# One decoder layer on one core: weight differences skipped at three token groups, a score bank for one group of transposes, output weight casts moved behind mixer parts

## The chip, the cores and the metric

The kernel runs on one core of a Trainium2 chip (trn2). The metric is the device time of one execution in microseconds (us). Five engines work side by side, each through its own instructions in a fixed order: PE (TensorE, matrix products), DVE (VectorE), ACT (ScalarE), POOL (GpSimd) and SP (SyncE, which here issues all the DMA transfers). An engine that must wait for another stands still, with everything that is queued behind the waiting instruction.

## The reference

The layer takes 1024 tokens of width 1024, puts 16 meta tokens ahead of them and computes, in fp32:

```python
h = concatenate([meta, x])                       # 1040 x 1024
a = rmsnorm(h, ln_mix_pre)
dq, dk, dv, hq, hf, hi, hg = split(a @ w_in)     # 28 column tiles of 128
y_diff = diff_attention(dq, dk, dv, ...)         # 4 heads, two softmaxes each: p0 - lam * p1, times v
y_hgrn = hgrn2(hq, hf, hi, hg, ...)              # 4 heads, gated linear recurrence with decay f
h = h + rmsnorm(concatenate([y_diff, y_hgrn]) @ w_out, ln_mix_post)
u = conv3(rmsnorm(h, ln_ffn_pre) @ w_up) + b     # causal convolution over 3 tokens, 2 x 2816 channels
h = h + rmsnorm((gelu(u[gate]) * u[up]) @ w_down, ln_ffn_post)
return h[16:]
```

## The kernel before

Each fp32 operand of a product is split into a rounded high part (a cast on ACT) and the low remainder (a subtraction on DVE or POOL), and three products stand for one: high x high, high x low, low x high. The tokens lie in 9 blocks (block 0 has 16 tokens, the others 128), in three groups of three blocks.

The mixer part runs head by head. PE's instructions keep the order in which the program writes them; the other engines' instructions are ordered by the scheduler. For head h, `interleave` (L57) mixes two streams. The dense stream (`dense`, L755) computes projections: for each column tile and each token group 24 products (8 slices of 128 rows, three products each). The side stream is either attention of head h (`attn`) or the recurrence of head h (`hgrn_head`). So there are two kinds of phase: in the first, four tiles of the recurrence's projections (hf, hq, hi, hg) run beside attention; in the second, with `wide` set, three tiles of the next head's attention projections (dq, dk, dv) run beside the recurrence.

Before each token group, `dense` also takes one step of a second side stream, `down_sums` (L194). It prepares differences of blocks of w_down for a Strassen-like product much later: for each of 11 slices it loads four 256 KB tiles (tag "wd", five buffers), and makes four subtractions on DVE (tiles named wd3, wd12, wd22, wd21), each followed by a store to a DRAM scratch tensor, tsc. A slice takes six steps: two that only pass time and four with a subtraction. All 11 slices take 66 steps; the loops offer 4 x 12 steps in the first kind of phase and 3 x 9 in the second, 75.

In attention, `scores(i)` makes the products S (two PSUM banks, tag "S", two such pairs) and for the last block also E (tag "m", two single banks). ACT exponentiates them into pb. `values(i)` turns the difference of the two softmaxes, pb, by PE transposes: four 128 x 128 blocks go to one PSUM tile, pt, in bank tag "m" (L695), and are copied to SBUF as at (by DVE for even pieces, by ACT for odd ones); the first key block goes to az. `apply(i)` multiplies them with v into pa (tag "m"). Blocks 4 to 7 have two such pieces, block 8 has three.

In the recurrence, DVE multiplies decay factors into q (kept in the mix tiles) and k (tile kr) level by level, PE makes the products of each level (pl), and after level 7 PE transposes kr (pk, L518) for the state update.

After the last head, `out_first` (L1036) computes the first half of the output projection while the recurrence of head 3 runs beside it: for token block i, the mixer parts mm (k slices 0 to 3 and 4 to 6) are split and multiplied with the weights wo0 into py, copied to y0. Beside that, the raw weights of the second half (wor1_k) are loaded and split (`load_wo`) into high (wh1 or woh1, ACT) and low (wl1 or wol1, DVE). The raw weights of the first half, wor0_3 to wor0_7, and those of the second half use the five "wd" buffers that the weight differences had.

Its order around the change, before:

```python
for n, i in enumerate(FIRST[2:]):
    for w in [nxt.pop(0) for _ in range((2, 2, 1, 1, 1, 1)[n])]:
        with tc.issue_after(V.last.ins):
            wo.append(load_wo(*w))
```

Here `issue_after` keeps an instruction behind a named one in the scheduler's order; `V.last` and `A.last` are the last DVE and ACT instructions written so far. SP issues its DMAs strictly in its own order, so a store that waits for DVE holds back every load behind it.

Of the kernel before, what the change touches and what calls it, by code (L numbers as in the profile page):

```python
# [26 lines left out]
NBLK = 9  # L27
# [10 lines left out]
def start(i):  # L38
    return 0 if i == 0 else META + P * (i - 1)


def rows(i):
    return META if i == 0 else P
# [44 lines left out]
def layer_kernel(ctx: ExitStack, tc: tile.TileContext, x, meta, table, lbl, gpre, gpost, win,  # L88
# [3 lines left out]
    V, A = Ordered(tc, nc.vector, state), Ordered(tc, nc.scalar, state)  # L92
# [56 lines left out]
    def ps_m(name):  # L149
        return pp.tile([P, 512], F32, tag="m", name=name)  # L150

    def ps_s(name):
        return pp.tile([P, 2, 512], F32, tag="S", name=name)

    def split(hi, lo, raw, eng=None):
        A.copy(hi, raw)
        (eng or G).tensor_tensor(lo, raw, hi.bitcast(F32), op=ALU.subtract)
# [18 lines left out]
    def mix(ks, t0, t1):  # L176
        g = 0 if t1 <= start(3) else 1 if t1 <= start(6) else 2
        base = start(GROUPS[g][0])
        return mixes[g][:, ks, t0 - base:t1 - base]
# [48 lines left out]
    def load_m(m, name, where=None, bufs=4):  # L228
        return [load_split(win[m][:, 512 * c: 512 * (c + 1)], f"{name}_{c}", where, bufs) for c in range(2)]

    def proj_group(g, parts, name, evac, wide=False):
        b0, b1 = GROUPS[g]
        t0, t1 = start(b0), start(b1 - 1) + P
        n = t1 - t0
        pt = ps_s(f"pi_{name}_{g}")[:, 0] if wide and g == 2 else ps_in(f"pi_{name}_{g}")
        for k in range(KD):
            yield from proj_step(pt[:, :n], parts, k, t0, t1, lambda: evac(g, b0, b1, t0, t1, pt[:, :n]))
# [171 lines left out]
    def flush():  # L409
        while late:  # L410
            to_nat(*late.pop(0))
# [212 lines left out]
    def attn(h, tens):  # L624
# [61 lines left out]
        def values(i):  # L686
            r = rows(i)
            q0 = start(i)
            W = q0 + r
            nm = f"{h}_{i}"  # L690
            pb = pend.pop(i)
            pieces = [list(range(j, min(j + 4, i + 1))) for j in range(0, i + 1, 4)]
            ats = []
            for pi, blks in enumerate(pieces):
                pt = ps_m(f"pt{nm}_{pi}")  # L695
                at = ap_.tile([P, len(blks) if pi == 2 else 4, P], F32, tag=f"at{pi // 2}", name=f"at{nm}_{pi}", bufs=2 - pi // 2)
                for jj, j in enumerate(blks):
                    b = rows(j) if i == 0 else P
                    T.transpose(pt[:b, jj * r:(jj + 1) * r], pb[:r, 0, start(j):start(j) + b], ident[:r, :r])
                pv = pt.rearrange("p (j q) -> p j q", j=4)[:, :, :r] if r == P else None  # L700
                n0 = len(blks)
                if pi == 0:
                    A.copy(az[i % 2][:META, :r], pt[:META, :r])
                lo = 1 if pi == 0 else 0
                if n0 > lo:
                    with tc.issue_after(pend["low"].ins) if i == NBLK - 2 else nullcontext():
                        (A.copy if pi % 2 else V.tensor_copy)(at[:, lo:n0], pv[:, lo:n0])
                ats.append(at)
                yield 0.8 if i < 4 else 0.6
            pend["ats"] = ats, pieces  # L710
# [47 lines left out]
    def dense(tiles, preload=None, side=iter(()), wide=False):  # L758
        parts = preload
        for idx, (m, name, evac) in enumerate(tiles):  # L760
            if parts is None:
                parts = load_m(m, name)
            nxt = load_m(tiles[idx + 1][0], tiles[idx + 1][1]) if idx + 1 < len(tiles) else None
            for g in range(3):
                next(side, None)
                for step, c in enumerate(proj_group(g, parts, name, evac, wide)):
                    if step == 8:
                        flush()
                    yield c
            parts = nxt  # L770
# [28 lines left out]
    pt = ps_m("pg")  # L799
# [146 lines left out]
    def load_wr(n, k):  # L946
        raw = (wp.tile([P, 512], F32, tag="wr", name=f"wor{n}_{k}", bufs=3) if n == 0 and k < 3
               else wsp.tile([P, 512], F32, tag="wd", name=f"wor{n}_{k}"))
        last_load.append(SY.dma_start(raw, wout[P * k: P * (k + 1), 512 * n: 512 * (n + 1)]))
        return n, k, raw  # L950

    def load_wo(n, k, raw):
        if k < 2:
            where, tag, bufs = wp, ("wh", "wl"), 4
        elif n == 0 and k < KD - 1:
            where, tag, bufs = w0p, ("woh", "wol"), KD - 3
        else:
            where, tag, bufs = w1p, ("woh", "wol"), KD - 1
        hi, lo = (where.tile([P, 512], F32R, tag=t, name=f"{t}{n}_{k}", bufs=bufs) for t in tag)
        split(hi, lo, raw, V if n or k else G)  # L960
        return hi, lo

    def tok(i):
        return (2, 14) if i == 0 else (P, start(i))

    def mix_split(i, k0, k1):
        r, t0 = tok(i)
        src = mix(slice(k0, k1), t0, t0 + r)
        if i < 2:
            hi, lo = (kept[:, 0, k0:k1], kept[:, 1, k0:k1]) if i else (m0[:, k0:k1, 0:2], m0[:, k0:k1, 32:34])  # L970
        elif k1 - k0 == 1:
            m = mlp.tile([P, 2, 1, P], F32R, tag="m1", name=f"mm{i}_{k0}", bufs=7)
            hi, lo = m[:, 0], m[:, 1]
        else:
            m = map_.tile([P, 2, k1 - k0, P], F32R, tag="mm", name=f"mm{i}_{k0}")
            hi, lo = m[:, 0], m[:, 1]
        A.copy(hi, src)
        V.tensor_tensor(lo, src, hi.bitcast(F32), op=ALU.subtract)
        if i > 1 and k1 < KD:
            for c in range(k0 // 2, (k1 + 1) // 2):  # L980
                ka, kb = max(k0, 2 * c), min(k1, 2 * c + 2)
                SY.dma_start(msc[i, c][:, :, P * (ka - 2 * c):P * (kb - 2 * c)],
                             m[:, :, ka - k0:kb - k0].bitcast(F32).rearrange("p l k t -> p l (k t)"))
        return hi, lo, k0, k1, r

    def out_part(sp_, py, wo, first, last, ks=None):
        mh, ml, k0, k1, r = sp_
        for k in ks or range(k0, k1):
            hi, lo = wo[k]
            j = k - k0  # L990
            T.matmul(py[:r], mh[:, j, :r], hi, start=(first and j == 0), stop=False)  # L991
            yield 216
            T.matmul(py[:r], mh[:, j, :r], lo, start=False, stop=False)
            yield 216
            T.matmul(py[:r], ml[:, j, :r], hi, start=False, stop=(last and k == k1 - 1))
            yield 216
# [12 lines left out]
    wo = []  # L1009
# [29 lines left out]
    def out_first():  # L1039
        pys = [ps_s(f"py0_{i}")[:, 0] for i in FIRST[:2]]  # L1040
        for ks in ((0, 1), (2, 3)):
            for j in range(2):
                yield from out_part(sps[j], pys[j], wo0, ks[0] == 0, False, ks)
        sqs = [mix_split(i, 4, 7) for i in FIRST[:2]]
        for j in range(2):
            yield from out_part(sqs[j], pys[j], wo0, False, True)
            if j == 0:
                sp_ = mix_split(FIRST[2], 0, 4)
            A.copy(y0[:, FIRST[j]], pys[j])
        nxt = [load_wr(1, k) for k in range(4)]  # L1050
        for n, i in enumerate(FIRST[2:]):
            for w in [nxt.pop(0) for _ in range((2, 2, 1, 1, 1, 1)[n])]:
                with tc.issue_after(V.last.ins):
                    wo.append(load_wo(*w))
            nxt += [load_wr(1, k) for k in ((4,), (5,), (6,), (7,), (), ())[n]]
            if n == 3:
                ahead.extend(mix_load(2, c) for c in range(4))
            py = ps_in(f"py0_{i}")
            sq_ = mix_split(i, 4, 7)
            yield from out_part(sp_, py, wo0, True, False)  # L1060
            if i != FIRST[-1]:
                sp_ = mix_split(FIRST[n + 3], 0, 4)
            yield from out_part(sq_, py, wo0, False, True)
            A.copy(y0[:, i], py)
        py = ps_in("py0_0")
        yield from out_meta(py, wo0, 0, 7, 6)
        A.copy(y0[:2, 0], py[32:34])
        V.tensor_tensor(y0[:2, 0], y0[:2, 0], py[:2], op=ALU.add)
        while 0 not in finished:
            yield None  # L1070
        for p in range(3):
            pre_last[p] = mix_split(p, 7, 8)
        for p in range(3):
            yield from out_last(p)
# [172 lines left out]
    for n, i in enumerate(order):  # L1247
# [9 lines left out]
        nxt = []  # L1257
# [507 lines left out]
```

## Time and profile before

| what | value |
|---|---|
| median of 3 runs | 1296.62 us (1295.83 to 1296.99) |
| the profiled execution | 1296.41 us, of which 1294.6 us from the first instruction to the last |
| PE busy | 1269.1 us (98%), so 25.5 us of idle |
| DVE, ACT, POOL busy | 916.8 us (71%), 689.2 us (53%), 408.7 us (32%) |
| granted TensorE clock | 0.999 |
| mixer with projections | up to about 514 us |
| output projection, first half beside recurrence 3 | about 514 to 576 us |

The page gives, for each group of instructions, its busy time, the mean duration and the idle time of its engine just before, with what ended it. In the timeline a row is: start, length, engine, line, operation, output<-inputs, shape, count, and in brackets the idle time of the engine before it and the instruction whose end released it. Helper functions carry most DVE and ACT instructions, so these rows have L54, and one reads them by their tile names.

### The profile page before, as it was taken

How to read it: one execution, taken by the hardware profiler on the slowest of the kernel's cores; microseconds unless marked ns; L12 is line 12 of the kernel's file. 1: busy time of each engine (PE TensorE's matmuls, PEld its weight loads, DVE VectorE, ACT ScalarE, POOL GpSimd, SP SyncE). 2: the span in 40 equal slices, each digit the busy share in tenths (PEclk: the TensorE clock that was granted, in tenths of full speed). 3: DMA queues.
4: the chain of work that ended last, by engine and by line, in shares of the span. 5: the costliest groups of instructions: out<-in, count | busy, mean ns of one | idle time of the engine just before them, and what ended most of it. 6: DMA issues, size and time to landing. Idle time of an engine off the chain costs nothing.

```text
span 1294.6 us, 26319 instructions
## 1 busy us (share of the span) xinstructions
PE 1269.1 (98%) x10236; PEld 1181.0 (91%) x10236; DVE 916.8 (71%) x1581; ACT 689.2 (53%) x1672; POOL 408.7 (32%) x322
## 2 busy tenths in 40 slices
PE   7999999999999999999999999999999999999997
PEld 6899999999999999777899999999999998888886
DVE  7566657575757565737887787787787786697587
ACT  7465347544654566446666455455445454454454
POOL 3211212021212020022154766766766730010020
PEclk9999999999999999999999999999999999999999
DMA  6222323122323311727612322222222236955363
GB/s 222 92 89 66 105 76 115 54 99 98 99 86 100 98 42 32 259 102 233 223 58 83 106 83 81 83 83 76 85 86 75 84 103 216 343 197 171 90 211 122
DMA packets 84371, 153.07 MB, mean 118 GB/s; under 512 B 9571, under 2 KB 19843, under 8 KB 84246
## 3 DMA queue, kind: packets, MB, share of 16 engines
q1 hardware_dynamic: 84246, 151.39, 35.1%
q8 instruction: 80, 1.31, 0.4%
q14 instruction: 45, 0.37, 0.1%
HBM read 112.69 MB, written 38.67 MB: 117 GB/s over the span
## 4 chain that ended last, share of the span: by engine, by line
PE 53%; DVE 2%; ACT 1%; DMA 0%; issue 0%; DVEq 0%; SPq 0%
PE pd L1576 5%; PE pd L1577 5%; PE pd L1575 5%; PE pb L1376 4%; PE pb L1377 4%; PE pb L1378 4%; PE pa L1377 3%; PE pa L1376 3%; PE pa L1378 3%; PE pc L1376 3%; PE pc L1378 3%; PE pc L1377 3%; PE pq L1353 2%; PE pq L1354 2%; PE pq L1355 2%; PE py L991 1%
## 5 line engine op out<-in xcount | busy, mean ns | idle before, releaser
L1376 PE MATMUL pb<-t,uh 128*128 128x258 f32 (+1 forms) x456 | 127.4, 279 | 0.7 <-DVE u L54 0.7
L1377 PE MATMUL pb<-t,uh 128*128 128x258 f32 (+1 forms) x456 | 127.3, 279 | 0.0
L1378 PE MATMUL pb<-t,ul 128*128 128x258 f32 (+1 forms) x456 | 127.2, 279 | 0.0
L1576 PE MATMUL pd<-wl,gh 128*128 128x512 f32 (+1 forms) x314 | 120.7, 384 | 0.4 <-DVE wl L54 0.3
L1577 PE MATMUL pd<-wh,gl 128*128 128x512 f32 (+1 forms) x314 | 120.9, 385 | 0.0
L1575 PE MATMUL pd<-wh,gh 128*128 128x512 f32 (+1 forms) x314 | 120.6, 384 | 0.0
L54 DVE SCALAR_TENSOR_TENSOR c<-uu,cwt,c 128x512 f32<-128x512 f32 x88 | 95.0, 1079 | 22.3 <-ACT c L54 21.4
L1325 POOL TENSOR_TENSOR c<-c,c 128x512 f32<-128x512 f32 x44 | 64.5, 1465 | 127.4 <-ACT c L54 108.6
L54 DVE SCALAR_TENSOR_TENSOR c<-ug,cwt,c 128x512 f32<-128x512 f32 x88 | 84.0, 955 | 6.6 <-ACT c L54 5.9
L1376 PEld LDWEIGHTS pb<-t,uh 128*128 128x128 f32 x456 | 85.8, 188 | 1.1 <-DVE u L54 1.1
L1377 PEld LDWEIGHTS pb<-t,uh 128*128 128x128 f32 x456 | 85.9, 188 | 0.0
L1378 PEld LDWEIGHTS pb<-t,ul 128*128 128x128 f32 x456 | 85.8, 188 | 0.0
L1377 PE MATMUL pa<-t,uh 128*128 128x256 f32 (+1 forms) x304 | 85.3, 281 | 0.0
L1378 PE MATMUL pa<-t,ul 128*128 128x256 f32 (+1 forms) x304 | 85.2, 280 | 0.0
L1376 PE MATMUL pa<-t,uh 128*128 128x256 f32 (+1 forms) x304 | 85.2, 280 | 0.0
L1378 PE MATMUL pc<-t,ul 128*128 128x256 f32 x304 | 83.9, 276 | 0.0
L1376 PE MATMUL pc<-t,uh 128*128 128x256 f32 x304 | 83.9, 276 | 0.0
L1377 PE MATMUL pc<-t,uh 128*128 128x256 f32 x304 | 83.9, 276 | 0.0
L1576 PEld LDWEIGHTS pd<-wl,gh 128*128 128x128 f32 x314 | 58.9, 188 | 13.8 <-DVE wl L54 1.5
L1577 PEld LDWEIGHTS pd<-wh,gl 128*128 128x128 f32 x314 | 59.0, 188 | 11.9
L1575 PEld LDWEIGHTS pd<-wh,gh 128*128 128x128 f32 x314 | 59.0, 188 | 11.8
L54 ACT ACTIVATE c<-ug,cbt,cwt 128x512 f32<-128x512 f32 x44 | 35.9, 816 | 44.0 <-issue 26.2
(411 smaller groups left out, 4289.3 us busy)
## 6 DMA issues: line engine op xcount, KB each, us to landing
ra<-in_wup_dram SPq DMA_DIRECT2D x76, 256.0 KB, 2.6
wd<-in_wdown_dram SPq DMA_DIRECT2D x44, 256.0 KB, 3.2
tsc<-wd SPq DMA_DIRECT2D x44, 256.0 KB, 2.2
gsc<-c SPq DMA_DIRECT2D x44, 256.0 KB, 2.0
wi<-tsc SPq DMA_DIRECT2D x44, 256.0 KB, 2.9
gi<-gsc SPq DMA_DIRECT2D x33, 256.0 KB, 3.7
wi<-in_wdown_dram SPq DMA_DIRECT2D x33, 256.0 KB, 3.3
msc<-mm SPq DMA_DIRECT2D x21, 256.0 KB, 3.3
```

Source lines behind the costliest of these rows:

```text
L54: ins = call(*args, **kw)
L991: T.matmul(py[:r], mh[:, j, :r], hi, start=(first and j == 0), stop=False)
L1325: G.tensor_tensor(cg, cg, cu, op=ALU.mult)
L1353: T.matmul(pt, hi[:, s], th[:, k], start=(kh + k == 0), stop=False)
L1354: T.matmul(pt, hi[:, s], tl[:, k], start=False, stop=False)
L1355: T.matmul(pt, lo[:, s], th[:, k], start=False, stop=(kh == 1 and k == 3))
L1376: T.matmul(pt, hi[:, s], th[:, k], start=(first and k == 0), stop=False, skip_group_check=True)
L1377: T.matmul(pt, hi[:, s], tl[:, k], start=False, stop=False, skip_group_check=True)
L1378: T.matmul(pt, lo[:, s], th[:, k], start=False, stop=(k == 3), skip_group_check=True)
L1575: T.matmul(py, gh[:, s], wh, start=(k == 0 and pr not in (3, 7)), stop=False, skip_group_check=True)
L1576: T.matmul(py, gh[:, s], wl, start=False, stop=False, skip_group_check=True)
L1577: T.matmul(py, gl[:, s], wh, start=False, stop=(k == NH - 1), skip_group_check=True)
```

## The change

There are three edits. First, in the second kind of phase (`wide`), `dense` takes no step of the weight differences before the token groups numbered 4, 5 and 6 of 9. This takes nine steps out of 75 and leaves the 66 that are needed, so the differences end with the last token group of head 3's first kind of phase. Second, the transposes of piece 1 of block 7 (NBLK - 2) go into the first half of a score pair (tag "S") and no longer into an "m" bank. Third, in `out_first` the splits of the second half's weights are written behind the next block's mixer part and behind the first products of the present block, and are kept behind the last DVE and the last ACT instruction; the loads of wor1_4 to wor1_7 are written earlier by one or more blocks in the table of loads.

```diff
-                pt = ps_m(f"pt{nm}_{pi}")
+                pt = ps_s(f"pt{nm}_{pi}")[:, 0] if (i, pi) == (NBLK - 2, 1) else ps_m(f"pt{nm}_{pi}")
...
             for g in range(3):
-                next(side, None)
+                if not (wide and 4 <= 3 * idx + g <= 6):
+                    next(side, None)
                 for step, c in enumerate(proj_group(g, parts, name, evac, wide)):
...
         for n, i in enumerate(FIRST[2:]):
-            for w in [nxt.pop(0) for _ in range((2, 2, 1, 1, 1, 1)[n])]:
-                with tc.issue_after(V.last.ins):
-                    wo.append(load_wo(*w))
-            nxt += [load_wr(1, k) for k in ((4,), (5,), (6,), (7,), (), ())[n]]
+            nxt += [load_wr(1, k) for k in ((), (4, 5), (6, 7), (), (), ())[n]]
...
             yield from out_part(sp_, py, wo0, True, False)
             if i != FIRST[-1]:
                 sp_ = mix_split(FIRST[n + 3], 0, 4)
+            for w in [nxt.pop(0) for _ in range((2, 2, 1, 1, 1, 1)[n])]:
+                with tc.issue_after(V.last.ins), tc.issue_after(A.last.ins):
+                    wo.append(load_wo(*w))
             yield from out_part(sq_, py, wo0, False, True)
```

Three places show how the instructions move. The last number in each name is a running buffer number. The first place is PE's order in attention of head 1, around piece 1 of block 7 (pt1_7_1) and the products that use it (pa1_7). Before, with the waits of each instruction:

```order
L247 MATMUL pi_hg1_0_3011<-ahi0_106,wl_hg1_0_2740 128x272 [waits Pool_49]
L699 MATMUL pt1_7_1_3015<-ident_73,pb1_7_2830 128x128 [waits DVE_49]
L699 MATMUL pt1_7_1_3015<-ident_73,pb1_7_2830 128x128 x3
...
L724 MATMUL pa1_7_3027<-avn1_1587,az1_130 128x128 [waits Activation_49]
L724 MATMUL pa1_7_3027<-avn1_1587,at1_7_0_2992 128x128 x3
L724 MATMUL pa1_7_3027<-avn1_1587,at1_7_1_3016 128x128 [waits Activation_49]
```

Now:

```order
L247 MATMUL pi_hg1_0_2998<-ahi0_106,wl_hg1_0_2729 128x272 [waits Pool_49]
L699 MATMUL pt1_7_1_3002<-ident_73,pb1_7_2824 128x128 x4
...
L724 MATMUL pa1_7_3014<-avn1_1587,az1_130 128x128 [waits DVE_49]
L724 MATMUL pa1_7_3014<-avn1_1587,at1_7_0_2986 128x128 x3
L724 MATMUL pa1_7_3014<-avn1_1587,at1_7_1_3003 128x128 [waits Activation_49]
```

The order of the products is the same; the transposes pt1_7_1 no longer wait for DVE, and pa1_7 waits for DVE where it waited for ACT.

The second place is DVE's order in the recurrence of head 0, levels 6 and 7, ahead of PE's transposes of kr. Before:

```order
L54 TENSOR_TENSOR kl1_126<-pi_dk1_1_1973,k1_1_1586 64x384
L54 TENSOR_TENSOR wd21_2_1620<-wd21_2_1620,wd22_2_1618 128x512
L54 COPY am_736<-pl0_6_2053 32x8x32 x2
L54 TENSOR_TENSOR mix0_99<-mix0_99,tt0_1638 128x2x64
L54 TENSOR_TENSOR mix1_100<-mix1_100,tt0_1638 128x3x64
L54 TENSOR_TENSOR kr0_739<-kr0_739,tt0_1638 128x8x64
L54 TENSOR_TENSOR mix2_101<-mix2_101,tt0_1638 128x3x64
```

Now:

```order
L54 TENSOR_TENSOR kl1_126<-pi_dk1_1_1971,k1_1_1586 64x384
L54 COPY am_736<-pl0_6_2049 32x8x32 x2
L54 TENSOR_TENSOR mix0_99<-mix0_99,tt0_1638 128x2x64
L54 TENSOR_TENSOR mix1_100<-mix1_100,tt0_1638 128x3x64
L54 TENSOR_TENSOR kr0_739<-kr0_739,tt0_1638 128x8x64
L54 TENSOR_TENSOR mix2_101<-mix2_101,tt0_1638 128x3x64
L54 COPY am_736<-pl0_7_2087 64x8x64
L54 TENSOR_TENSOR kl0_125<-pi_dk1_2_2044,k0_1_1585 64x384
L54 TENSOR_TENSOR kl1_126<-pi_dk1_2_2044,k1_1_1586 64x384
L54 TENSOR_TENSOR wd22_2_1618<-wd22_2_1618,wd12_2_1616 128x512
```

The difference wd21_2 is gone from ahead of the copies am and the products with mix and kr; another one, wd22_2, comes behind kl, and wd21_2 itself later still.

The third place is the output projection. ACT's order there, before:

```order
L54 CAST woh1_6_6934<-wor1_6_6767 128x512
L54 COPY y0_6308<-py0_4_6562 128x512
L54 CAST mm6_4_6770<-mix2_101 128x384
L54 CAST mm7_0_6829<-mix2_101 128x512
L54 CAST woh1_7_7013<-wor1_7_6871 128x512
L54 COPY y0_6308<-py0_5_6690 128x512
L54 CAST mm7_4_6882<-mix2_101 128x384
```

Now:

```order
L54 CAST woh1_3_6749<-wor1_3_6550 128x512
L54 COPY y0_6308<-py0_4_6552 128x512
L54 CAST mm6_4_6768<-mix2_101 128x384
L54 CAST mm7_0_6827<-mix2_101 128x512
L54 CAST woh1_4_6832<-wor1_4_6678 128x512
L54 COPY y0_6308<-py0_5_6682 128x512
L54 CAST mm7_4_6878<-mix2_101 128x384
```

At the same point among the mixer parts ACT now casts weight 4 where it cast weight 7. And SP's order at the end of head 3's attention, before:

```order
L212 DMA tsc_93<-wd21_10_5285 128x512
L949 DMA wor0_6_6346<-in_wout_dram 128x512
L949 DMA wor0_7_6348<-in_wout_dram 128x512
L163 DMA wr_hg3_1_5896<-in_win_dram 128x512
L949 DMA wor0_0_6334<-in_wout_dram 128x512
```

Now:

```order
L212 DMA tsc_93<-wd22_10_5889 128x512
L950 DMA wor0_5_6344<-in_wout_dram 128x512
L212 DMA tsc_93<-wd21_10_5891 128x512
L950 DMA wor0_6_6346<-in_wout_dram 128x512
L950 DMA wor0_7_6348<-in_wout_dram 128x512
L934 DMA gpo0_6312<-in_gpost_dram 128x512
L983 DMA msc_94<-mm2_0_6350 256x1x256 x2
```

The last weight differences and the loads of wor0_6 and wor0_7 now stand behind all loads of head 3's projection weights, directly ahead of the output projection's own transfers; on DVE the subtraction of wd21_10 now stands behind the gate of the last projection tile's second token group.

## The prediction

> **What bounds the kernel now.** I read the page's busy times first, then PE's waits, then the timelines around the three edits.
>
> ```profile
> span 1294.6 us, 26319 instructions
> PE 1269.1 (98%) x10236; PEld 1181.0 (91%) x10236; DVE 916.8 (71%) x1581; ACT 689.2 (53%) x1672; POOL 408.7 (32%) x322
> ```
>
> PE is idle for 1294.6 - 1269.1 = 25.5 us in all, and it keeps its order and its products. So the change can only move idle time of PE: it gains where a wait goes, and loses where a new one comes. The waits of PE by line (total us, times, longest) that stand at the three edits:
>
> ```profile
> PE pk L518 <- DVE kr L54: 2.4, 2, 1.2
> PE pt L699 <- DVE at L54: 2.3, 4, 1.0
> PE pl L456 <- DVE kr L54: 0.6, 1, 0.6
> PE pl L462 <- DVE mix L54: 0.2, 1, 0.2
> ```
>
> Together that is 5.5 us, the most that the change can give.
>
> **The score bank.** The transposes of piece 1 of block 7 wait once in each head, until DVE has copied piece 0 (at) out of the bank that they reuse. PE's rows of heads 0 and 1 (head 2 has the rest of the 2.3 beside head 3's row further down, 0.52):
>
> ```profile
> 119.68 0.66 PE L699 MATMUL pt<-ident,pb 128*128 128x128 f32 x4 [0.24 <-DVE at L54]
> ...
> 246.49 0.66 PE L699 MATMUL pt<-ident,pb 128*128 128x128 f32 x4 [0.52 <-DVE at L54]
> ...
> 247.94 1.73 PE L724 MATMUL pa<-avn,at 128*128 128x128 f32 x14
> ```
>
> In a bank of its own this wait is gone, but the products pa behind still need the copy of piece 1, which ACT makes, and ACT doesn't get to it earlier: it is busy with an exponential until then.
>
> ```profile
> 246.81 0.66 ACT L54 ACTIVATE pb<-E,ast 128x512 f32<-128x512 f32 x1
> 247.47 0.56 ACT L54 COPY at<-pt 128x512 f32<-128x512 f32 x1
> ```
>
> The copy ends at 247.47 + 0.56 = 248.03. Of the 14 products pa, six use piece 0; the seventh stands at 247.94 + 6 x 1.73/14 = 248.68. Moved 0.52 earlier it would start at 248.16, so 0.13 us of room is left and head 1 keeps all of its 0.52. I take the same for head 2, and all of the 0.24 in head 0, where less is moved. In head 3 more is moved:
>
> ```profile
> 497.24 0.66 PE L699 MATMUL pt<-ident,pb 128*128 128x128 f32 x4 [1.03 <-DVE at L54]
> 498.10 0.58 ACT L54 COPY at<-pt 128x512 f32<-128x512 f32 x1
> 498.59 0.61 PE L724 MATMUL pa<-avn,at 128*128 128x128 f32 x4
> ```
>
> The seventh product stands at about 498.59 + 6 x 0.12 = 499.31, the copy ends at 498.68 plus a hand-over that I put at 0.1; so 0.53 of the 1.03 is gained and a wait of 0.5 on ACT is left. **Term 1: 0.24 + 0.52 + 0.52 + 0.53 = 1.81 us**, with bounds of 0 (the copies decide everywhere) and 2.31.
>
> **The differences left out.** A subtraction of the weight differences (wd) stands in DVE's queue just ahead of the work that PE's transposes pk wait for. Head 0, DVE and then PE:
>
> ```profile
> 166.96 1.35 DVE L54 TENSOR_TENSOR wd<-wd,wd 128x512 f32<-128x512 f32 x1
> 168.34 0.85 DVE L54 COPY am<-pl 32x256 f32<-32x256 f32 x2
> 169.22 1.63 DVE L54 TENSOR_TENSOR mix<-mix,tt 128x128 f32<-128x128 f32 x2
> 170.77 0.68 DVE L54 TENSOR_TENSOR kr<-kr,tt 128x512 f32<-128x512 f32 x1
> ...
> 171.50 0.55 PE L518 MATMUL pk<-ident,kr 128*128 128x128 f32 x3 [1.20 <-DVE kr L54]
> ```
>
> Two of these rows are stretched, and POOL's rows say why: its weight splits run at the same time.
>
> ```profile
> 166.49 1.27 POOL L157 TENSOR_TENSOR wl_hf<-wr_hf,wh_hf 128x512 fp32r<-128x512 f32 x1 [11.03 <-ACT wh_hf L54]
> 169.15 1.28 POOL L157 TENSOR_TENSOR wl_hf<-wr_hf,wh_hf 128x512 fp32r<-128x512 f32 x1 [1.39 <-ACT wh_hf L54]
> ```
>
> Without wd the copies am start at 166.96 and end at 167.81. The mix pair follows, for which I take 0.56 us from head 1 (next fence), to 168.37, and kr with 0.68 ends at 169.05. Without its wait pk would have come at 171.50 - 1.20 = 170.30, so 1.25 us of room is left, and kr would be through before POOL's second split at 169.15, with 0.78 between the two starts. Head 1 shows the chain where POOL doesn't meet it:
>
> ```profile
> 294.55 0.56 DVE L54 TENSOR_TENSOR mix<-mix,tt 128x128 f32<-128x128 f32 x2
> 295.02 0.69 DVE L54 TENSOR_TENSOR kr<-kr,tt 128x512 f32<-128x512 f32 x1
> 296.00 0.49 PE L518 MATMUL pk<-ident,kr 128*128 128x128 f32 x3
> ```
>
> Here pk has no wait. Heads 0 and 2 have the two waits of the list above; **term 2: 2 x 1.20 = 2.40 us**, with bounds of 0 (kr meets POOL and another operation) and 2.40. The number of subtractions is unchanged; nine of the steps fall elsewhere, most into attention. There DVE has pauses, as just behind the copy of at in head 1:
>
> ```profile
> 247.60 0.16 DVE L54 TENSOR_TENSOR ast<-ast 128x1 f32<-128x1 f32 x1 [1.16 <-ACT pb L54]
> ```
>
> A subtraction stands there now; 0.68 fits into 1.16, and I cost it at nothing. With POOL beside it, it would take 1.35, 0.19 more than the pause: over three heads, at most 0.6 us.
>
> The Trainium skill (SBUF — State Buffer, section "SBUF: two separate sides") says that DVE and POOL share a pair of ports as an exclusive lock: an operation of DVE with two SBUF inputs and one of POOL don't share it, and whichever starts first keeps it to its end. The 1.35 for wd against 0.68 for kr agrees. By this rule alone the order of starts decides, and the 0.78 between kr and POOL's split would be all that protects term 2.
>
> **The casts in the output projection.** ACT stands behind the load of wor1_7, and with it a copy y and the cast mm of block 7; DVE waits for mm, and kr comes late for PE:
>
> ```profile
> 538.10 0.39 PE L995 MATMUL py<-woh,mm 128*128 128x512 f32 x1
> ...
> 540.67 0.62 ACT L54 CAST woh<-wor 128x512 fp32r<-128x512 f32 x1 [4.46 <-DMA wor<-in_wout_dram]
> 541.67 0.52 ACT L54 CAST mm<-mix 128x384 fp32r<-128x384 f32 x1
> 542.22 0.56 DVE L54 TENSOR_TENSOR mm<-mix,mm 128x384 fp32r<-128x384 f32 x1 [2.37 <-ACT mm L54]
> 542.70 0.68 DVE L54 TENSOR_TENSOR kr<-kr,tt 128x512 f32<-128x512 f32 x1
> 543.43 0.76 PE L456 MATMUL pl<-mix,kr 128*32 128x32 f32 x22 [0.60 <-DVE kr L54]
> ...
> 528.53 0.94 SPq L949 DMA_DIRECT2D wor<-in_wout_dram  x2
> ```
>
> Now wor1_4 is cast there. It takes the place among SP's loads that wor1_5 had, issued at 528.5 (last row); even with the longest landing of these loads (6.3 us, quoted below) it is there at 534.8. Then only PE's product of 538.10 holds y: y from 538.5 to 539.1, mm to 539.6, the low part to 540.2, kr to 540.9, and PE needs it at 543.43 - 0.60 = 542.83. The 0.60 go, with 1.9 of room. The smaller wait comes from the same kind of cast, further ahead:
>
> ```profile
> 521.78 0.62 ACT L54 CAST wh<-wor 128x512 fp32r<-128x512 f32 x1 [2.95 <-DMA wor<-in_wout_dram]
> ...
> 527.44 0.80 PE L462 MATMUL pl<-mix,kr 128*32 128x16 f32 x63 [0.23 <-DVE mix L54]
> ```
>
> This cast and the next now stand behind mm of block 5; they, and a wait of up to 2.95, go from ahead of the mixer parts. If only the two casts count, mm comes 2 x 0.62 = 1.2 us earlier, more than the 0.23. **Term 3: 0.83 us**, bounds 0 and 0.83.
>
> **The sum.** 1.81 + 2.40 + 0.83 = 5.04 us off the profiled execution of 1296.41, whose span is 1294.6 with 1.8 around it; it lies 0.21 under the median of 1296.62. From the median: 1291.6 us.
>
> **Rivals.** *POOL meets kr.* If kr starts behind 169.15, it waits until 170.43 and ends at 171.11, and pk waits 0.81 of its 1.20 in both heads: 1291.6 + 1.6 = 1293.2. For it: two of four DVE rows there are stretched already. Against it: 0.78 us of room, and head 1.
>
> *Copies in place of banks.* The 0.13 of room in heads 1 and 2 is no more than a hand-over, and the moved subtractions stand ahead of copies of at. Then term 1 is lost: 1293.4. Against it: the 0.13 is positive, and a hand-over that is longer costs only its excess.
>
> *The last differences hold up the output projection (the slower side).* The last subtraction comes behind the gate of head 3's last projection tile, on DVE until about 511.3. The load of wor0_7 needs the buffer and waits for that store to land. Before, the same step was long over:
>
> ```profile
> 450.21 0.33 SPq L212 DMA_DIRECT2D tsc<-wd  x1
> 450.63 2.22 SPq L949 DMA_DIRECT2D wor<-in_wout_dram  x2
> ...
> DMA to landing us min/median/max: 2.0/2.6/5.4
> ...
> DMA to landing us min/median/max: 2.5/2.9/6.3
> ...
> 514.77 1.15 ACT L54 CAST woh<-wor 128x512 fp32r<-128x512 f32 x2
> ...
> 522.71 0.40 PE L991 MATMUL py<-woh,mm 128*128 128x512 f32 x1
> ```
>
> (The two landing rows are those of tsc and of wor.) With medians wor0_7 is there at 511.3 + 2.6 + 2.9 = 516.8. On ACT three operations (0.6, 0.5, 0.5) from the cast of woh0_7 lead to the mm that PE needs at 522.71, so a landing up to about 521 costs nothing. With both maxima it is 523.0: 2 us late for mm, and DVE's whole queue behind it is 6.2 us later than by the medians. If half of that reaches PE beside the 2, and all loads of the second half behind them on SP come late once more, the loss is about 5.8, and the time 1297.4; every further us of the landing costs one. Against it: it needs both maxima.
>
> *Nothing comes of it:* a later stage takes the time back, 1296.4. Against it: behind the projection PE's waits are short and are released by work that itself follows PE.
>
> **Chances.** The forecast 0.60, with its own range of 1290.8 to 1292.8; POOL meets kr 0.08; copies 0.12; last differences 0.10; nothing 0.10. A measurement can tell 0.2%, 2.6 us, from no change, so faster is a time below 1294.0. Faster: 0.60 + 0.08 + two thirds of 0.12 (the rest, where it meets another loss) = 0.76. Slower, above 1299.2: half of the 0.10 of the last differences, where a landing goes past the maxima: 0.05. The remaining 0.19 is the same. The range runs from 1290.6 (all of the 5.5, and 0.5 for the spread of the runs) to 1295.4, short of the two last rivals.
>
> **What would show it.** Right: in PE's waits no pk L518 on DVE, pt L699 gone but for about 0.5 on ACT at pa in head 3, pl L456 gone; ACT without the 4.46 on wor; PE's busy time unchanged at 1269. Wrong: kr in heads 0 and 2 of 1.3 us beside POOL; a wait of pa on ACT in heads 1 and 2; ACT waiting at woh0_7 beyond 521 and PE behind it; or the idle time of PE down by 5 at 576 us and back at the end.

## The result and the profile after

| | before | changed |
|---|---|---|
| median of 6 runs | 1297.16 us (1295.83 to 1299.53) | 1291.46 us (1290.85 to 1293.14) |
| ratio, 95% interval | | 0.9955 [0.9945, 0.9965] |
| profiled span | 1294.6 us | 1289.7 us |
| PE busy | 1269.1 us | 1268.4 us |

The change makes the kernel 0.45% faster, 5.7 us by the medians (the three runs known at the forecast had a median of 1296.62). The same kernel run again later gave 1291.19 us and 0.9953 [0.9941, 0.9966]. PE's waits after, those that bear on the change:

```profile
PE py L992 <- DMA mp<-msc: 1.3, 2, 1.0
PE pa L724 <- ACT at L54: 0.5, 2, 0.3
```

The list has no wait of pk, pt or pl any more (2.4, 2.3, 0.6 and 0.2 before). Two entries are there in their place: pa waits for ACT's copy, 0.5 in all, and py for the mixer parts mp, 1.3 where it was 0.6.

First the place of the skipped difference, head 0. DVE, then POOL, then PE:

```profile
165.89 0.85 DVE L54 COPY am<-pl 32x256 f32<-32x256 f32 x2
166.76 0.56 DVE L54 TENSOR_TENSOR mix<-mix,tt 128x128 f32<-128x128 f32 x2
167.24 0.69 DVE L54 TENSOR_TENSOR kr<-kr,tt 128x512 f32<-128x512 f32 x1
...
165.44 1.28 POOL L157 TENSOR_TENSOR wl_hf<-wr_hf,wh_hf 128x512 fp32r<-128x512 f32 x1 [10.49 <-ACT wh_hf L54]
168.63 1.28 POOL L157 TENSOR_TENSOR wl_hf<-wr_hf,wh_hf 128x512 fp32r<-128x512 f32 x1 [1.91 <-ACT wh_hf L54]
...
169.50 0.29 PE L245 MATMUL pi_dv<-alo,wh_dv 128*128 128x272 f32 x1
169.63 0.49 PE L518 MATMUL pk<-ident,kr 128*128 128x128 f32 x3
```

The mix pair takes 0.56 us (1.63 before), kr starts 1.39 us ahead of POOL's second split, is done at 167.93, and pk follows the product ahead of it without a pause.

Second, the products pa of block 7 in head 3, PE and ACT:

```profile
493.83 0.39 PE L724 MATMUL pa<-avn,at 128*128 128x128 f32 x2
494.56 0.71 PE L724 MATMUL pa<-avn,at 128*128 128x128 f32 x4 [0.34 <-ACT at L54]
...
493.93 0.58 ACT L54 COPY at<-pt 128x512 f32<-128x512 f32 x1
```

The transposes pt no longer wait, and ACT's copy, which ends at 494.51, now decides. Third, ACT in the output projection, where it had stood 4.46 us for wor1_7:

```profile
533.52 0.59 ACT L54 COPY y<-py 128x512 f32<-128x512 f32 x1 [1.79 <-PE py L996]
534.00 0.51 ACT L54 CAST mm<-mix 128x384 fp32r<-128x384 f32 x1
```

The copy y waits for PE's own product, and the cast mm follows at once.

Since PE's instructions stand in the same order, the start of the same instruction in both profiles shows where the time went. The lead is the start before minus the start after:

| instruction on PE | before | after | lead |
|---|---|---|---|
| pt of block 7, head 0 | 119.68 | 119.22 | 0.46 |
| pk, head 0 | 171.50 | 169.63 | 1.87 |
| pi_hg behind pa of block 7, head 1 | 249.42 | 247.06 | 2.36 |
| pk, head 2 | 421.74 | 417.62 | 4.12 |
| pi_hg behind pa of block 7, head 3 | 500.07 | 495.48 | 4.59 |
| pl of level 5, output projection | 543.43 | 537.75 | 5.68 |
| product py behind that pl | 546.23 | 540.35 | 5.88 |
| py on mp of block 7 | 624.15 | 619.14 | 5.01 |
| span | 1294.6 | 1289.7 | 4.9 |

The lead grows at the places of the three edits, to 5.9 us, and 0.9 of it is given back at the mixer parts.

### The profile page after: what moved, and what is told of

Its sections match the earlier page's. It is cut to its first block, busy times and chain, and to the rows that moved or that the text cites. A ratio compares the mean times of both kernels' runs of the same rounds, so it can differ in the third digit from the quotient of the medians.

```text
span 1289.7 us, 26320 instructions
## 1 busy us (share of the span) xinstructions
PE 1268.4 (98%) x10236; PEld 1181.4 (92%) x10236; DVE 911.8 (71%) x1581; ACT 690.1 (54%) x1672; POOL 411.1 (32%) x322
## 4 chain that ended last, share of the span: by engine, by line
PE 90%; DVE 5%; ACT 2%; DMA 1%; issue 1%; POOL 0%; SPq 0%; DVEq 0%; ACTq 0%; POOLq 0%
PE pd L1577 5%; PE pd L1578 5%; PE pd L1576 5%; PE pb L1377 4%; PE pb L1378 4%; PE pb L1379 4%; PE pa L724 3%; PE pa L1378 3%; PE pa L1379 3%; PE pa L1377 3%; PE pc L1378 3%; PE pc L1379 3%; PE pc L1377 3%; PE py L992 2%; PE py L996 2%; PE py L994 2%
## 5 line engine op out<-in xcount | busy, mean ns | idle before, releaser
L1201 POOL TENSOR_TENSOR ws<-ra,ra 128x512 f32<-128x512 f32 x38 | 56.9, 1498 | 8.5 <-DMA ra<-in_wup_dram 5.7
```

The lines of the kernel that those rows point to most:

```text
L1201: G.tensor_tensor(sums[nm], a, b, op=op)
```

## The experiments

### Each part alone

```diff
e1_skip   + if not (wide and 4 <= 3 * idx + g <= 6):
          +     next(side, None)
e2_bank   + pt = ps_s(f"pt{nm}_{pi}")[:, 0] if (i, pi) == (NBLK - 2, 1) else ps_m(f"pt{nm}_{pi}")
e3_casts  - (load_wo of the second half ahead of the block's mixer parts)
          + (load_wo behind the next mix_split, with issue_after(V.last) and issue_after(A.last);
          +  and the changed table of loads of wor1_4 to wor1_7)
```

> Only the skipped steps (groups 4, 5 and 6), on the kernel before. The sum's theory: the two waits of pk on kr (1.20 each) are gone and nothing else moves, 2.4 us less than before, 2.7 with what PE loses around each wait by the offsets of the two traces. The rival 'moved subtractions hold up attention': with the old bank the copy of piece 0 still decides, and a subtraction now stands in front of DVE's work there, so the waits of pt grow and the gain is under 1.5 us. The rival 'last differences': PE waits near 522 us for mm behind the cast of woh0_7 and the time is not under that of before.

> Only the score bank, on the kernel before. The sum's theory: the four waits of pt (2.31) go and about 0.5 comes back as a wait of pa on ACT's copy of piece 1 in head 3, 1.8 us less. The rival 'copies in place of banks': ACT's copy decides in heads 1 to 3 and the gain is no more than 0.5 us; then waits of pa on ACT of about 0.3 to 0.5 with a lengthened product after each are to be seen in three heads. In the trace of the change I read something between: waits of 0.14, 0.16 and 0.34, and 1.9 us net; so 1.3 to 2.0.

> Only the casts of the output projection, on the kernel before. The sum's theory: the waits of 0.23 and 0.60 go, 0.8 us less (1.1 by the offsets of the two traces between 500 and 575 us). What came back later, the longer wait for mp: if it is caused by the casts or by the order of loads on SP, it stands here too (mp waits about 1.3 instead of 0.6 and the time is within 0.4 us of before); if it follows from PE's arriving 5 us earlier than before, or is only the spread of the DMA's durations, it is 0.3 to 0.9 here.

| part | median | ratio, 95% interval | waits gone (lead gained there, from the product ahead of the place to the products behind it) | PE's mp waits |
|---|---|---|---|---|
| skip | 1293.73 us | 0.9978 [0.9969, 0.9988] | pk, both (2.83) | 0.7 |
| bank | 1295.18 us | 0.9994 [0.9982, 1.0005] | pt, four (1.71, net of pa) | 0.7 |
| casts | 1295.98 us | 0.9994 [0.9985, 1.0003] | pl, both (1.27) | 2.1 |

The medians lie 3.0, 1.6 and 0.8 us under that of before (1296.76), 5.4 together. By time only the skip can be told from no change; by the traces each part takes away the waits that its term names. The casts alone lose their lead again at the mixer parts in this profile (2.1 us of waits). In the bank's run the copies take back a part, as the waits show:

```profile
PE pk L518 <- DVE kr L54: 2.4, 2, 1.2
PE pa L724 <- ACT at L54: 0.5, 2, 0.3
```

The waits of the output projection are less fixed than one profile makes them look. In the six kernels that have the old casts, pl L456 waits 0.6 (before), 1.0 (skip), 0 (bank), 1.1 and 0 and 0.6 (the next three kernels). In the kernel before its chain begins with ACT's wait for a load of wor, and the longest such wait of ACT there is 3.1 to 4.9 us in the six. Both waits of pl together make 0.4 to 1.3 us in these six, and neither is listed in any of the eight profiles with the new casts.

### POOL moved away from kr, the difference left in place

```diff
+            if lev == 7 and h < HEADS - 1:
+                held[h + 1] = G.tensor_copy(pad[:, :1], kr[:, META:META + 1])
...
-        split(hi, lo, raw)
+        with tc.issue_after(held[h].ins) if h else nullcontext():   # for the tile hf of heads 1 to 3
+            split(hi, lo, raw)
```

> The kernel before, with the weight difference left where it stands, and POOL made to wait for kr: a copy of one column of kr to an unused tile goes ahead of POOL's two weight splits in heads 0 to 2, which are otherwise the same. Theory that the waits of pk came from DVE's operations being stretched beside POOL's splits: wd takes 0.7 instead of 1.35, the mix pair 0.56 instead of 1.63, kr ends 0.5 before PE needs it, and the two waits of pk are gone with the subtraction still there: 2.4 to 2.7 us less than before. Rival, that the subtraction's own place is what costs (0.68 of queue ahead of kr, whoever runs beside): pk still waits 0.6 to 1.2 in heads 0 and 2, and the time is within 1.2 us of before.

DVE, POOL and PE in head 0:

```profile
167.10 0.70 DVE L54 TENSOR_TENSOR wd<-wd,wd 128x512 f32<-128x512 f32 x1
168.70 0.56 DVE L54 TENSOR_TENSOR mix<-mix,tt 128x128 f32<-128x128 f32 x2
169.18 0.69 DVE L54 TENSOR_TENSOR kr<-kr,tt 128x512 f32<-128x512 f32 x1
...
170.14 2.53 POOL L159 TENSOR_TENSOR wl_hf<-wr_hf,wh_hf 128x512 fp32r<-128x512 f32 x2
...
170.29 0.49 PE L524 MATMUL pk<-ident,kr 128*128 128x128 f32 x3
```

The subtraction stands where it stood, wd takes 0.70 instead of 1.35, the mix pair 0.56 instead of 1.63, and pk doesn't wait in any head. The time is 1295.18 us, 0.9991 [0.9982, 0.9999]; the lead gained at the two pk is 2.83 us as in the skip, of which this profile loses 1.7 later at pl (1.1, where 0.6 had been) and at mp (1.6). So by the rows the waits came from the meeting with POOL; the subtraction mattered because it took 0.7 us of room and met the first split. The time itself is only 1.6 us below before, where 2.4 to 2.7 were expected.

### Other groups left out

```diff
e5_skip5     + if not (wide and 3 * idx + g == 5):
e6_skip123   + if not (wide and 1 <= 3 * idx + g <= 3):
```

> Only group 5 is skipped, on the kernel before: three steps leave the recurrence's phases instead of nine, and the differences end in the middle of head 3's attention instead of at its last token group. If the gain of the skip comes from the one step that stands ahead of kr, all of it is here: the two waits of pk gone, 2.4 to 2.7 us less than before. If it needs the room of all nine steps, less than half of it is here.

> Groups 1, 2 and 3 are skipped instead of 4, 5 and 6, on the kernel before: as many steps leave the recurrence's phases, and the differences end as late, but a subtraction stands ahead of kr in heads 0, 1 and 2. Theory of the place: the waits of pk stay, 2 x 1.2, with a third of up to 1.2 in head 1 if POOL's split meets it there, so the time is 0 to 1.5 us above before. Rival, that it is the number of subtractions beside the recurrence that counts: as in the skip of 4, 5 and 6, 2.4 us or more below before.

| groups left out | median | ratio, 95% interval | pk waits | pl L462 waits |
|---|---|---|---|---|
| 5 | 1295.37 us | 0.9984 [0.9975, 0.9993] | none | 1.6, longest 1.1 |
| 1, 2, 3 | 1296.19 us | 0.9992 [0.9983, 1.0000] | none | 3.2, three of about 1.1 |

Group 5 is the step that stands ahead of kr, and leaving it out alone takes both waits of pk away (2.8 us of lead). But a new wait comes up in head 2. The second run was to keep the waits of pk, since a subtraction does stand ahead of kr there, and it did not. The kernel before shows why, in its own head 1, which had no wait either (DVE, then POOL):

```profile
292.28 1.36 DVE L54 TENSOR_TENSOR wd<-wd,wd 128x512 f32<-128x512 f32 x1
...
295.00 1.85 POOL L157 TENSOR_TENSOR wl_hf<-wr_hf,wh_hf 128x512 fp32r<-128x512 f32 x1 [1.91 <-ACT wh_hf L54]
```

A subtraction stands ahead of kr here too and is stretched beside POOL's first split. But the mix pair (294.55) is through before the second split comes, and kr, at 295.02 by its row, takes 0.69 while POOL takes 1.85. What heads 0 and 2 have besides, and what counts here, is one more subtraction, further ahead:

```profile
159.77 0.69 DVE L54 TENSOR_TENSOR wd<-wd,wd 128x512 f32<-128x512 f32 x1
```

With it kl starts 4.35 us ahead of the place where pk would come without a wait (165.80 against 170.15), without it 4.88 (291.12 against 296.00). Leaving out groups 1 to 3 takes this one away in heads 0 and 2, and all three heads then look as head 1 did: wd 1.35 or 1.36, kr 0.68 or 0.69 beside a split of 1.82 to 1.85, no wait. So by these runs a wait of pk needed three things, and taking away any one of them ended it: POOL's splits beside the chain, the subtraction of group 5, and the one further ahead. The skip of 4 to 6 takes both subtractions away.

The second run lost its time elsewhere. Level 3 of head 0 in it, DVE, POOL, PE:

```profile
153.69 1.78 DVE L54 TENSOR_TENSOR kr<-kr,t 128x520 f32<-128x520 f32 x1
156.64 0.30 DVE L54 TENSOR_TENSOR mix<-mix,t 128x136 f32<-128x136 f32 x1
...
153.06 0.49 POOL L426 TENSOR_TENSOR tt<-tt 128x16 f32<-128x16 f32 x2
153.51 1.41 POOL L157 TENSOR_TENSOR wl_dv<-wr_dv,wh_dv 128x512 fp32r<-128x512 f32 x1
...
157.08 0.59 PE L462 MATMUL pl<-mix,kr 128*32 128x16 f32 x50 [1.06 <-DVE mix L54]
```

The same place before:

```profile
153.61 0.70 DVE L54 TENSOR_TENSOR kr<-kr,t 128x520 f32<-128x520 f32 x1
...
153.72 1.75 POOL L157 TENSOR_TENSOR wl_dv<-wr_dv,wh_dv 128x512 fp32r<-128x512 f32 x1
```

Before, kr started 0.11 us ahead of POOL's split and POOL took 1.75; now POOL is 0.18 us ahead and kr takes 1.78, 1.1 more, and PE waits 1.06. Behind it is POOL's own order: in this kernel the scheduler put the first split of the tile dv behind three steps of the tree of decays (tt), where it had stood ahead of them. It did so in heads 0, 1 and 2 of this kernel and in head 2 alone of the one that leaves out group 5, which are the heads with the new wait. A subtraction taken out moves the meeting; it doesn't always remove it. The skip of 4 to 6 leaves POOL's order and the rows at level 3 as they were (kr 0.70, POOL 1.75).

It also makes the heads alike. A head's two phases had 12 + 9 = 21 steps, three and a half slices of six, so the pattern of subtractions shifted by half a slice from head to head, and heads 0 and 2 had the second subtraction and the wait while head 1 had neither. With 18 steps, three whole slices, every head has the same pattern; the skip of 1 to 3, which has 18 as well, repeats its loss at level 3 in all three.

### POOL put in front of kr

```diff
e10_pool   + (behind the first mix of level 7, on the changed kernel)
           + with tc.issue_after(G.tensor_copy(pad[:, :1], q(s9 - 1, s9)).ins):
           +     G.tensor_tensor(hold[:, 0], f, f, op=ALU.mult)
e11_hold   + (behind the copies am of level 6, on the changed kernel)
           + G.tensor_tensor(hold[:, 0], f, am.rearrange("p b c -> p (b c)")[:, :L], op=ALU.mult)
```

> The changed kernel, with an extra multiplication on POOL (128 x 1040, both inputs in SBUF, its result unused) that starts behind the first of the two mix operations ahead of kr in heads 0, 1 and 2, so just ahead of kr. It prices the rival 'POOL meets kr'. If DVE and POOL keep one another out for whole operations: kr waits until POOL is done, some 2.6 us after its start, ends near 0.8 us after PE needs it, and pk waits about 0.8 in three heads: 2.4 to 3.3 us above the changed kernel, and kr takes 2.5 us or more by the rows. If they share: kr takes at most 1.4, still ends before PE needs it, and the time is that of the changed kernel.

> As the run with an extra multiplication on POOL, but started earlier: it now waits for the copies am of level 6, so it begins beside the mix pair, ahead of kr, in heads 0, 1 and 2 (its result is unused). In that run POOL began 0.08 us after kr, kr took 0.69, and the next operation of DVE took 2.08 instead of 0.35, until POOL was through. If the first to start keeps the other out, kr or the mix operation ahead of it now waits for POOL's 2.4 us, kr ends 0.7 to 0.9 after PE wants it, and pk waits that long in three heads: 2 to 3.3 us above the changed kernel. If only the order of kr and POOL at that place happened to be bad for the operation behind, kr takes 0.7 and the time is that of the change.

The first of the two missed its place by 0.08 us. DVE and POOL in it:

```profile
167.63 0.69 DVE L54 TENSOR_TENSOR kr<-kr,tt 128x512 f32<-128x512 f32 x1
168.23 2.08 DVE L54 TENSOR_TENSOR mix<-mix,tt 128x192 f32<-128x192 f32 x1
...
167.71 2.38 POOL L482 TENSOR_TENSOR hold<-f 128x1040 f32<-128x1040 f32 x1
```

kr had begun and was untouched; the next operation, 0.35 us in the change, ended at 170.31, right behind POOL's 170.09. PE doesn't need that one soon, and the time is 1291.24 us. The second got there first; DVE, POOL, PE:

```profile
166.91 2.80 DVE L54 TENSOR_TENSOR mix<-mix,tt 128x128 f32<-128x128 f32 x2
169.64 1.75 DVE L54 TENSOR_TENSOR kr<-kr,tt 128x512 f32<-128x512 f32 x1
...
166.96 2.54 POOL L492 TENSOR_TENSOR hold<-f,am 128x1040 f32<-128x1040 f32 x1
169.46 1.38 POOL L159 TENSOR_TENSOR wl_hf<-wr_hf,wh_hf 128x512 fp32r<-128x512 f32 x1
...
171.45 0.55 PE L523 MATMUL pk<-ident,kr 128*128 128x128 f32 x3 [1.51 <-DVE kr L54]
```

The first mix had begun 0.05 us ahead; the second waited for POOL's 2.54 us, and kr, behind it, for POOL's next split too. pk waits about 1.5 in each of three heads (4.5 in all), and the time is 1296.76 us, 5.6 us over the change run beside it, almost all of its gain. The expectation of 0.7 to 0.9 a head left out the second split: two operations of POOL with almost no gap between them shut DVE out twice.

### What came back, and two attempts to get more

```diff
e8_later   - (store of hsc and load of the next xh at c == 2, ahead of the products)
           + if c == 2 and n:    # behind mix_load(i + 1, 2)
           +     store_h(before, done)
           +     if n + 1 < NBLK:
           +         x_in(order[n + 1])
e7_at_dve  - (A.copy if pi % 2 else V.tensor_copy)(at[:, lo:n0], pv[:, lo:n0])
           + (A.copy if pi % 2 and i != NBLK - 2 else V.tensor_copy)(at[:, lo:n0], pv[:, lo:n0])
e9_both    (both of these); a12_change (the changed kernel again, beside them)
```

> The changed kernel, with SP's store of a finished token block (hsc) and the load of the next x block written behind the third load of mixer parts (mp, k slices 4 and 5) instead of ahead of it. What came back of the gain stands at two places where mp's third load was issued behind that store, which waits for DVE: mp of blocks 5 and 7. If SP's order is the cause, both waits go (0.3 and 1.0 in the trace of the change, 1.3 to 1.7 us with what PE loses around them). If the transfer itself is what is late, mp waits stay and the time is that of the change.

> The changed kernel again, as it is, for the two that follow it: 1291 to 1292 us, and waits of mp of 0.6 to 2.1 us in the profile, at blocks 5 and 7.

> The changed kernel, with the copy of piece 1 of block 7 on DVE instead of ACT, where it stands behind a weight difference. The trace of the change has the products pa 0.4 us late in heads 1 to 3 behind ACT's copy (waits of 0.14, 0.16 and 0.34 and a longer product behind each). If ACT's exponential in front of that copy is the limit, DVE has the copy done before PE comes, though the difference is stretched beside POOL (1.25 in the trace): no wait of pa, 1.2 us less than the changed kernel. If the copy then holds up DVE's work on the last block (its sums and pb, which PE's last transposes need), this is taken back: waits of pt or of pa of block 8, and the time is that of the change or above it.

> The changed kernel with both: the copy of piece 1 on DVE, and SP's store of a finished block behind the third load of mixer parts. If the two add up, 1.2 us from the one and 0.6 to 1.1 from the other (1.1 was the difference of the two profiled spans): 1.8 to 2.3 us less than the changed kernel. If a later stage limits (the last block's a2s, for which PE waited 0.6 in the run with the store moved), less than 1.2.

| kernel | median | ratio to before, 95% interval | PE's waits on mp | profiled span |
|---|---|---|---|---|
| the change again | 1291.19 us | 0.9953 [0.9941, 0.9966] | 0.6 | 1289.4 us |
| store later | 1290.81 us | 0.9951 [0.9938, 0.9963] | none | 1288.6 us |
| copy on DVE | 1291.33 us | 0.9956 [0.9944, 0.9969] | 0.6 | 1289.4 us |
| both | 1291.00 us | 0.9954 [0.9941, 0.9968] | none | 1288.6 us |

The waits on mp stand at the third load of blocks 5 and 7, which SP issued behind the store of a finished block. SP and PE in the change:

```profile
613.37 0.32 SPq L1132 DMA_DIRECT2D hsc<-xh  x1
613.78 1.36 SPq L1035 DMA_DIRECT2D mp<-msc  x2
...
619.14 0.50 PE L992 MATMUL py<-woh,mp 128*128 128x512 f32 x1 [0.98 <-DMA mp<-msc]
```

With the store behind that load both waits are gone, in both kernels that have it, so SP's order lets them arise; of the 1.3 to 1.7 us expected from it, 0.8 is seen in the spans. A part comes back when the last block is turned: in that run PE waits for DVE there.

```profile
PE pa L1147 <- DVE a2s L54: 0.6, 1, 0.6
```

The profiled span is those 0.8 us shorter than that of the change beside it, and the same holds for the pair with the copy on DVE; by time neither pair can be told apart. How long mp is late differs between profiles of one kernel (1.3 and 0.6 for the change), between the kernels with the old casts (0.6 to 2.0), and between those with the new casts and the old place of the store (0.3 to 2.1). The run of the casts alone was to blame the casts if mp waited about 1.3 there; it waited 2.1, but two kernels without the casts waited 1.6 and 2.0, so that line decides nothing. What came back in the first profile lies within this spread; a cost of the three edits is not shown.

The copy on DVE gains nothing by time, where 1.2 us less than the change was expected. In heads 1 and 2 the scheduler put it behind a weight difference, which POOL stretches there. DVE and PE in head 1:

```profile
244.71 1.26 DVE L54 TENSOR_TENSOR wd<-wd,wd 128x512 f32<-128x512 f32 x1
245.89 0.68 DVE L54 COPY at<-pt 128x512 f32<-128x512 f32 x1
...
246.62 0.60 PE L724 MATMUL pa<-avn,at 128*128 128x128 f32 x3 [0.32 <-DVE at L54]
```

PE waits for DVE's copy there in place of ACT's. In head 3, where no split stands beside the difference (0.68), no wait of pa is left, and the lead gained is 0.72 where it was 0.42. No version was measurably faster than the change.

## Why the prediction held, step by step

The forecast was 1291.6 us and 5.04 us of gain; the measured median is 1291.46, and the lead behind the first half of the output projection 5.9, more than the 5.5 that the prediction called the most the change can give. The waits that it named are gone, and the mechanism held. That the time agrees within 0.2 us is in part luck: the three places gave 5.8, 0.8 more than the sum; 1.0 of the lead was lost again behind them, which the sum doesn't have, so that the profiled execution gained 4.9 (1296.41 to 1291.52); and the median of before rose from 1296.62 to 1297.16 with the later runs.

**Term 1, 1.81 us forecast, 1.73 by the leads** (0.46, 0.43, 0.42 and 0.42 in heads 0 to 3, each net of pa). The sum is near, the parts are not: head 0 gave twice its 0.24, the others 0.1 less each. The copy on ACT became the limit in three heads, not in one, and a wait of pa in heads 1 and 2 was one of the prediction's own signs of being wrong. Head 2, PE and ACT:

```profile
370.12 1.05 PE L724 MATMUL pa<-avn,at 128*128 128x128 f32 x7 [0.16 <-ACT at L54]
...
369.51 0.56 ACT L54 COPY at<-pt 128x512 f32<-128x512 f32 x1
```

The room of 0.13 us was wrong because the products moved further than 0.52: the first product pa of block 7 came 0.83 us earlier in head 1 and 0.85 in head 2, against the lead ahead of pt, for the reason given under the next term. The hand-over from ACT's copy to PE, put at 0.1 from no row, is 0.05 here (370.07 to 370.12) and in head 3. In head 3 a wait of 0.5 was foreseen and one of 0.34 came.

**Term 2, 2.40 forecast, 2.83 by the leads.** The mechanism was right, and the run with POOL moved away shows it. One reading behind it was wrong: POOL does meet kr in head 1 of the kernel before, as the rows above show. The size was short because a wait costs PE more than the idle time in the row. PE before, ahead of pk (the row of pk with its 1.20 at 171.50 is quoted in the prediction):

```profile
169.89 0.29 PE L243 MATMUL pi_dv<-ahi,wh_dv 128*128 128x272 f32 x1
170.02 0.28 PE L245 MATMUL pi_dv<-alo,wh_dv 128*128 128x272 f32 x1
```

Products are 0.29 us long but start every 0.13: they overlap. The 1.20 counts from the end of the last one, 170.30; without a wait pk would have started at 170.15, as it does after the change, 0.13 behind its predecessor. So the wait cost 1.35, and the first transposes behind it took 0.55 instead of 0.49: 1.41 in all, 2.83 in both heads. The places of the other waits gained more than the idle time as well (0.46 for 0.24, 0.30 for 0.23, 0.87 for 0.60). That explains most of what the sum left out at terms 2 and 3; in term 1 the waits of pa took it back.

**Term 3, 0.83 forecast, 1.28 by the leads.** Both waits went, and with them the 4.46 us of ACT's. That their size is itself a draw (0 to 1.1 us for the larger in kernels with the old casts) was not in the forecast; and 0.11 of the 1.28 lies between the two waits, where it stands in kernels without the new casts too.

**The rivals.** *POOL meets kr* did not happen; an extra operation of POOL that brought it about cost about 1.5 us in each of three heads, about twice the 0.81 that was priced. The protection was larger than the forecast's 0.78 us: 1.39 by the rows, since the other subtraction, further ahead, was gone too and kl came 0.53 earlier. The prediction had counted only the one beside kr. *Copies in place of banks* happened in part, with waits of 0.34 us at most in a head. *The last differences* stayed hidden:

```profile
506.57 0.33 SPq L212 DMA_DIRECT2D tsc<-wd  x1
506.99 2.16 SPq L950 DMA_DIRECT2D wor<-in_wout_dram  x2
...
511.62 0.61 ACT L54 CAST woh<-wor 128x512 fp32r<-128x512 f32 x1
```

woh0_7 was cast at 511.62, or 516.2 in the times of before at a lead of 4.6, so the load had landed by then (516.8 was reckoned); nothing waited. What a late landing would cost was not tried. *Nothing comes of it* has a true part behind the output projection's first half: mp gave back 0.9 in one profile and nothing in the next, where other waits further on took 1.0 (a lead of 6.1 us behind mp, 5.1 at the end).

The Trainium skill's rule (SBUF — State Buffer, section "SBUF: two separate sides") that the first to start keeps the shared ports to its end agrees with the runs: 0.11 us ahead kr took 0.70, 0.18 us behind it took 1.78. Only closer than that the rows can't tell who was first: in head 1 of the kernel before kr's row starts 0.02 us behind POOL's, and it was POOL that was held.

## What to carry to other kernels

Where two engines shut one another out, look for the few tenths of a microsecond that decide who starts first, and read both queues at that place: removing an operation can remove the meeting, move it, or turn it round, and the operation that matters can stand further ahead than the one beside the wait. A periodic side job whose period doesn't divide the loop's steps gives the passes different patterns; making it divide makes one good pass good for all, or one bad pass bad for all, as the skip of 1 to 3 did. To size a removed wait of PE, compare starts of products, not ends: here a removed wait gave back up to 0.3 us more than its idle time.

## What was not expected of the hardware

An operation of DVE that comes 0.2 us behind one of POOL is held until POOL's is through (kr, 0.70 alone, took 1.78 behind a split of 1.41), and the next operation of POOL can slip in between two of DVE: behind 2.54 us of POOL, kr of 0.69 us still took 1.75. In the other direction POOL pays too: its split takes 1.75 us behind a running kr, against 1.28 alone. And the DMA waits of one and the same program differ by up to 0.7 us from profile to profile (mp 1.3 and 0.6), almost as much as the smallest term of the sum.
